# Attention logits of two heads in two row halves of the array, running sums and mask as a bias tile

## The chip, the core and the metric

One core of a Trainium2 chip runs the whole kernel. Five engines work side by side, each in the order of its own instruction queue: TensorE (PE in the profile; its weight loads are listed apart as PEld), VectorE (DVE), ScalarE (ACT), GpSimd (POOL) and SyncE (SP, which here only issues transfers). They wait for each other by semaphores. The metric is the device time of one execution in microseconds (us); less is better. "Before" is the median of 3 runs.

## What is computed

A decoder trunk of two layers over 256 tokens of width 1024, all in float32: a recurrent (RG-LRU) layer first, then a layer of forgetting attention. Each layer has a SwiGLU FFN of half weight in front of its mixer and another behind it. The part at issue is the attention of the second layer: 16 heads of 64, queries in two blocks of 128, and a running sum `c` of log forget gates per head that is added for the query and subtracted for the key.

```python
def shared_kv(h, g, w_kv, w_f, b_f):
    hn = rms_norm(h, g)
    kv = (hn @ w_kv).reshape(Bn, S, 2, N_HEADS, HEAD_DIM)
    k, v = ...
    log_f = jax.nn.log_sigmoid((hn @ w_f + b_f).astype(jnp.float32))
    c = jnp.cumsum(log_f, axis=1).transpose(0, 2, 1)

def forgetting_attention(xq, w_q, w_o, k, v, c):
    q = (xq @ w_q).reshape(...).transpose(0, 2, 1, 3) * (HEAD_DIM ** -0.5)
    for blk in range(S // Q_BLOCK):
        logits = jnp.einsum('bhqd,bhkd->bhqk', q[:, :, q0:end], k[:, :, :end])
        logits = logits + c[:, :, q0:end, None] - c[:, :, None, :end]
        logits = jnp.where(kpos[None, :] <= qpos[:, None], logits, -jnp.inf)
        p = jax.nn.softmax(logits, axis=-1)
        outs.append(jnp.einsum('bhqk,bhkd->bhqd', p, v[:, :, :end]))
    return o @ w_o
```

## The kernel before

**Tokens and products.** The 256 tokens are two tiles of 128, `t` = 0 and 1. Weights come in units of up to 128x1024 floats by transfers that SyncE issues (`load_raw`, 5 `raw` buffers). Each unit is split into a high part `whi` on ScalarE (L173) and a low part `wlo` on VectorE (L177), with 9 buffers each (`WB`). Each product is three fp32r matmuls, high by high, high by low and low by high (`mm3`, L183 to L185). TensorE's order is written out by hand: `run` and `ATT_ORDER` decide which unit of which tile comes next. The other engines' orders come from a scheduler, except where `keep_in_program_order` or `high_priority` is said; the GpSimd work of the attention is kept in program order.

**PSUM.** Eight banks: four `mm` for the products, two `gt` (logits, the gates of the recurrent layer, the transposes of the stream, the running sums), two `tr` (other transposes).

**Keys, queries and the running sums.** The keys are projected right after the recurrent layer, among the units of the next FFN, the queries after that FFN. `heads_T` scales a 128x512 piece of a projection (`htok`, L954, VectorE), transposes it in four pieces (L959, TensorE) and writes even heads by ScalarE (L962) and odd heads by VectorE (L963), so that each head has its 64 features on partitions 0 to 63 of `kT` or `qT`. Two more rows carry the sums: row 64 of `kT` is 1 and row 65 the sum at the key; row 64 of `qT` is the sum at the query and row 65 is -1. So a product over 66 rows gives the logits with both terms. The sums come from `running`: the negated log gates `lf` times a triangle of -1 (`triu`, and `mone` for the first tile's total), copied to `c` (L993) and moved to the row of `kT` by a small transfer on GpSimd's queue (L994). `att_rows` moves `c` and `mone` to the rows of `qT` (L947, L948). The mask is one tile `cmask` of 0 and -1e30.

**The attention of one tile.** Groups of `per` heads: 4 of 128 keys for `t` = 0, 2 of 256 keys for `t` = 1, so each group's logits fill one bank. Four steps per group, each at the place that `ATT_ORDER` gives it (`l0` is the logits of a group of tile 0; a bare digit is a unit of weights for that tile):

- `l`, `logits`: the products into one `gt` bank (L1063), the mask added on the diagonal block (L1064) and the negative maximum (L1066) on VectorE, then per head an exponential with its sum on ScalarE (L1071)
- `n`, `norm`: reciprocal of the sums (L1077) and the product with it (L1078) on VectorE
- `t`, `turn`: four transposes (L1084) and a copy to `pT` (L1086)
- `v`, `values`: the products with `v`, two heads side by side in column halves of the array (L1098), and after eight heads the split of the output (L1104, L1105)

**The recurrent layer's gates** (`gw_unit`, L761) are block-diagonal fp32 products over tiles of 126 rows. The parts that cross a tile's edge are products over rows 0 to 63 and over rows 64 to 125, issued alternately into two banks. They are not touched by the change.

**GpSimd** also computes the two small steps of each RMS norm, `nv` (L198) and `rstd` (L200), whose results VectorE and ScalarE need as scales.

## Time and profile before

| | us |
|---|---|
| median of 3 runs | 987.98 (987.91 to 988.26) |
| profiled execution, its own time | 987.51 |
| its span, first to last instruction | 985.8 |
| logits products L1063, busy, by tile | 4.3 and 8.2 |
| mask and maximum on VectorE (L1064, L1066), busy, by tile | 5.5 and 8.9 |

The granted TensorE clock was 0.998 of full speed over the span.

How to read it: busy time is the time in which an engine executes an instruction. Matmuls are pipelined, so their busy times overlap; the chain of waits, which follows the work back from the last instruction, gives each piece of the path once. In a row of grouped instructions, `gt<-kT,qT` names the tile written and the tiles read, `66*128 66x256` the weights' rows and columns and the moving operand, `x32` the count. Behind the bar stand the busy time in us, the mean of one in ns, and the idle time before them with what ended it. An fp32 matmul of the program is two matmuls in the trace.

### The profile page before, as it was taken

To read this page: it belongs to the slowest core of one execution; us is meant where nothing else is said; L and a number is where in the kernel's file an instruction comes from. 1 tells how busy PE (TensorE), PEld (TensorE's weight loads), DVE (VectorE), ACT (ScalarE), POOL (GpSimd) and SP (SyncE) were. 2 spreads that over 40 slices of the span, in tenths; PEclk is the share of its full clock that TensorE was granted. 3 is DMA by queue.
4 is the path that set the end of the run, shared out by engine and by line. 5 is a ranking of instruction groups with operands and counts; after the bars stand their busy time and mean duration, and the time that the engine had idled before them with its cause. 6 is when DMAs were issued, how large, how long until landed. Compare 5 with 4: busy or idle time off the path is not lost.

```text
span 985.8 us, 13028 instructions
## 1 busy us (share of the span) xinstructions
PE 978.0 (99%) x4777; PEld 813.4 (83%) x4777; DVE 616.6 (63%) x791; ACT 530.1 (54%) x753; POOL 47.2 (5%) x92
## 2 busy tenths in 40 slices
PE   9999999999999999999999999999999999999997
PEld 6888888898978888888898888888888788888886
DVE  6666554678997555554686655554488876555542
ACT  7545443568986544443564444544366755444431
POOL 2400000100003000000100000000020000000000
PEclk9999999999999999999999999999999999999999
DMA  8787766565346877666567676665552467776631
GB/s 292 263 266 249 222 210 192 158 192 162 117 126 198 241 211 212 217 207 188 131 203 242 186 220 213 214 213 185 190 173 64 123 210 235 213 213 212 205 117 43
DMA packets 99558, 190.45 MB, mean 193 GB/s; under 512 B 12734, under 2 KB 32614, under 8 KB 99494
## 3 DMA queue, kind: packets, MB, share of 16 engines
q1 hardware_dynamic: 98054, 188.95, 61.3%
q8 instruction: 38, 0.62, 0.3%
q10 hardware_dynamic: 608, 0.53, 0.2%
q0 software_dynamic: 832, 0.12, 0.1%
q14 instruction: 26, 0.21, 0.1%
HBM read 176.95 MB, written 1.05 MB: 181 GB/s over the span
## 4 chain that ended last, share of the span: by engine, by line
PE 98%; issue 1%; DVE 1%; ACT 0%; POOL 0%; POOLq 0%; DVEq 0%; ACTq 0%
PE mm L183 29%; PE mm L185 29%; PE mm L184 28%; PE gt L761 2%; PE tr L525 1%; PE mm L1195 1%; PE gt L1063 1%; PE mm L190 1%; PE mm L191 1%; PE mm L192 1%; PE mm L1098 1%; PE tr L1084 1%; PE gt L214 1%; PE tr L127 0%; PE tr L959 0%
## 5 line engine op out<-in xcount | busy, mean ns | idle before, releaser
L177 DVE TENSOR_TENSOR wlo<-raw,whi 128x1024 fp32r<-128x1024 f32 (+5 forms) x329 | 395.3, 1207 | 268.3 <-ACT whi L173 266.1
L173 ACT ACTIVATE whi<-raw 128x1024 fp32r<-128x1024 f32 (+5 forms) x329 | 341.9, 1046 | 314.8 <-PE mm L185 260.2
L183 PE MATMUL mm<-whi,xhi 128*128 128x512 f32 (+1 forms) x768 | 301.2, 392 | 0.0
L185 PE MATMUL mm<-whi,xlo 128*128 128x512 f32 (+1 forms) x768 | 298.2, 388 | 0.3 <-DVE xlo L228 0.3
L184 PE MATMUL mm<-wlo,xhi 128*128 128x512 f32 (+1 forms) x768 | 297.9, 388 | 0.0
L185 PEld LDWEIGHTS mm<-whi,xlo 128*128 128x128 f32 x768 | 144.2, 188 | 30.7 <-DVE xlo L228 0.7
L183 PEld LDWEIGHTS mm<-whi,xhi 128*128 128x128 f32 x768 | 144.2, 188 | 29.4 <-issue 1.3
L184 PEld LDWEIGHTS mm<-wlo,xhi 128*128 128x128 f32 x768 | 144.3, 188 | 28.2 <-DVE wlo L177 0.3
L183 PE MATMUL mm<-whi,hhi 128*128 128x512 f32 x352 | 137.9, 392 | 0.0
L185 PE MATMUL mm<-whi,hlo 128*128 128x512 f32 x352 | 137.1, 389 | 0.0
L184 PE MATMUL mm<-wlo,hhi 128*128 128x512 f32 x352 | 137.0, 389 | 0.0
L185 PEld LDWEIGHTS mm<-whi,hlo 128*128 128x128 f32 x352 | 66.1, 188 | 13.9
L184 PEld LDWEIGHTS mm<-wlo,hhi 128*128 128x128 f32 x352 | 66.1, 188 | 13.3
L183 PEld LDWEIGHTS mm<-whi,hhi 128*128 128x128 f32 x352 | 66.1, 188 | 13.3
L510 DVE SCALAR_TENSOR_TENSOR prod<-mm,rstd,sil 128x512 f32<-128x512 f32 (+1 forms) x48 | 33.8, 705 | 35.2 <-PE mm L185 31.1
L498 ACT ACTIVATE sil<-mm,rstd 128x512 f32<-128x512 f32 (+1 forms) x48 | 31.2, 651 | 38.7 <-PE mm L185 34.2
L198 POOL TENSOR_SCALAR nv<-ss 128x1 f32<-128x1 f32 x22 | 9.6, 435 | 716.3 <-ACT junk L205 716.3
L529 ACT ACTIVATE hhi<-tr 128x512 fp32r<-128x512 f32 (+1 forms) x48 | 24.8, 558 | 13.8 <-PE tr L525 13.8
L205 ACT ACTIVATE junk<-mm 128x512 bf16<-128x512 f32 x24 | 14.3, 595 | 32.7 <-PE mm L185 32.6
L272 DVE TENSOR_TENSOR t<-mm,gb 128x512 f32<-128x512 f32 x24 | 16.1, 685 | 24.7 <-ACT junk L205 24.6
L530 DVE TENSOR_TENSOR hlo<-tr,hhi 128x512 fp32r<-128x512 f32 (+1 forms) x48 | 29.2, 640 | 2.6 <-ACT hhi L529 2.6
L183 PE MATMUL mm<-whi,zhi 128*128 128x340 f32 (+2 forms) x80 | 28.2, 353 | 0.0
(196 smaller groups left out, 885.8 us busy)
## 6 DMA issues: line engine op xcount, KB each, us to landing
raw<-in_ffn_w_down_dram SPq DMA_DIRECT2D x88, 512.0 KB
raw<-in_ffn_w_up_dram SPq DMA_DIRECT2D x80, 512.0 KB
raw<-in_ffn_w_gate_dram SPq DMA_DIRECT2D x78, 512.0 KB
prr<-prod SPq DMA_DIRECT2D x40, 256.0 KB
raw<-in_rg_w_in_dram SPq DMA_DIRECT2D x10, 504.0 KB
raw<-in_rg_w_out_dram SPq DMA_DIRECT2D x10, 504.0 KB
raw<-in_ffn_w_gate_dram SPq DMA_DIRECT2D x19, 256.0 KB
raw<-in_ffn_w_up_dram SPq DMA_DIRECT2D x16, 256.0 KB
```

What stands on the lines that cost most here:

```text
L173: up = nc.scalar.activation(hi[:parts, c:c + m], rawv[:, c:c + m], AF.Copy)
L177: nc.vector.tensor_tensor(lo[:parts, c:c + m], rawv[:, c:c + m], hi[:parts, c:c + m].bitcast(F32), ALU.subtract)
L183: nc.tensor.matmul(ps, xh, wh, start=first, stop=False)
L184: nc.tensor.matmul(ps, xh, wl, start=False, stop=False)
L185: nc.tensor.matmul(ps, xl, wh, start=False, stop=last)
L205: nc.scalar.activation(junk[:, :src.shape[1]], src, AF.Square, scale=f, accum_out=acc)
L272: nc.vector.tensor_tensor(t1[n], pf[n], gb[:, n * 512:(n + 1) * 512], ALU.mult)
L498: nc.scalar.activation(s[:, :nn], ps, AF.Silu, scale=rs[t][:, 0:1])
L510: nc.vector.scalar_tensor_tensor(pr[:, :nn], ps, rs[t][:, 0:1], s, ALU.mult, ALU.mult)
L529: nc.scalar.activation(hv, tp[:, :nn], AF.Copy)
L530: nc.vector.tensor_tensor(lv, tp[:, :nn], hv.bitcast(F32), ALU.subtract)
L761: nc.tensor.matmul(ps[j][:w, g * S:(g + 1) * S], wv[rows, o:o + w], xc[rows, k, :], start=start, stop=stop, skip_group_check=True)
```

## The change

- **Layout.** `kT` and `qT` keep what the transposes give: even heads on partitions 0 to 63, odd heads on 64 to 127, 8 columns of pairs in place of 16 heads. One ScalarE copy of 128x512 writes both, and VectorE's copy of odd heads is gone. The two rows for the sums are gone.
- **Logits.** Heads are taken alternately from the lower and the upper 64 rows, into two `gt` banks, one per half. A group takes both banks.
- **Bias.** `bias0` (128x16x128) and `bias1` (128x16x256) hold, for each query, head and key, the sum at the query less the sum at the key, and -1e30 where the key is later than the query. `lf` is the negated log gate, so the sums that go to the DRAM tile `crows` are negated. They come back broadcast to all partitions on GpSimd's queue, GpSimd subtracts `cq`, the negated sum at the query (one value per partition and head), and masks the last 128 columns with `affine_select`, four heads at a time. `bias0` is made in `running(0)`, `bias1` in `att_rows`.
- **Running sums.** `triu` is now +1, `mone` is a column `one`. `running` makes the sums twice: by rows of heads (`pc`, as before) and by partitions of tokens (`pq`, copied to `cq`).
- **One operation per head.** `tensor_tensor_reduce` on VectorE writes the negated sum of logits and bias to `pe` in SBUF and its minimum, which is the negated maximum, to `mx`. It is emitted as two instructions, the operation and a read of its accumulator. The exponential reads `pe` with scale -1 and bias `mx`.
- **Buffers.** The query's `htok` uses the `pT` buffers.

```diff
 def kv_tiles():
-        kv["kT"] = lp.tile([HA, NH, S], F32, name="kT")
+        kv["kT"] = lp.tile([P, NH // 2, S], F32, name="kT")
...
+        kv["bias0"] = lp.tile([P, NH, P], F32, name="bias0")
+        kv["rows"] = dram.tile([NH, S], F32, name="crows")
...
+    def bias_of(v, t, h0, hn):
+        keep = tc.keep_in_program_order
+        w = v.shape[2]
+        keep(nc.gpsimd.tensor_tensor(v, v, kv["cq"][t][:, h0:h0 + hn].unsqueeze(2).to_broadcast([P, hn, w]), ALU.subtract))
+        d = v[:, :, w - P:]
+        keep(nc.gpsimd.affine_select(out=d, in_=d, compare_op=ALU.is_ge, fill=NEG, base=0,
+                                     pattern=[[0, hn], [-1, P]], channel_multiplier=1))

     def att_rows():
         tc.keep_in_program_order(nc.scalar.activation(warm, mhalf, AF.Exp))
-        for t in range(2):
-            tc.keep_in_program_order(nc.gpsimd.dma_start(att["q"][t][HD:HD + 1, :, :], kv["c"][t]))
-            tc.keep_in_program_order(nc.gpsimd.dma_start(att["q"][t][HD + 1:HA, :, :], kv["mone"][:NH, :]))
+        v = att["bias1"]
+        tc.keep_in_program_order(nc.gpsimd.dma_start(v, kv["rows"].partition_broadcast(P)))
+        for h0 in range(0, NH, 4):
+            bias_of(v[:, h0:h0 + 4, :], 1, h0, 4)
...
             with tc.high_priority():
-                nc.scalar.activation(to[:, :, 0, :], tp[:HD, :].rearrange("p (a b) -> p a b", a=4), AF.Copy)
-                nc.vector.tensor_copy(to[:, :, 1, :], tp[HD:, :].rearrange("p (a b) -> p a b", a=4))
+                nc.scalar.activation(dst[:, 4 * n:4 * n + 4, :], tp.rearrange("p (a b) -> p a b", a=4), AF.Copy)
...
     def running(t):
-        pc = gtbank()
+        pc, pq = gtbank(), gtbank()
+        one = kv["one"].to_broadcast([P, P])
         if t == 1:
-            nc.tensor.matmul(pc[:NH, :P], kv["lf"][0], kv["mone"], start=True, stop=False)
+            nc.tensor.matmul(pc[:NH, :P], kv["lf"][0], one, start=True, stop=False)
         nc.tensor.matmul(pc[:NH, :P], kv["lf"][t], kv["triu"], start=t == 0, stop=True)
-        nc.vector.tensor_copy(kv["c"][t], pc[:NH, :P])
-        nc.gpsimd.dma_start(kv["kT"][HD + 1:HA, :, t * P:(t + 1) * P], kv["c"][t])
+        if t == 1:
+            nc.tensor.matmul(pq[:, :NH], one, kv["lf"][0], start=True, stop=False)
+        nc.tensor.matmul(pq[:, :NH], kv["triu"], kv["lf"][t], start=t == 0, stop=True)
+        ct = pools["f"].tile([NH, P], F32, name=f"c{t}")
+        nc.vector.tensor_copy(ct, pc[:NH, :P])
+        nc.vector.tensor_copy(kv["cq"][t], pq[:, :NH])
+        nc.gpsimd.dma_start(kv["rows"][:, t * P:(t + 1) * P], ct)
+        if t == 0:
+            nc.gpsimd.dma_start(kv["bias0"], kv["rows"][:, :P].partition_broadcast(P))
+            for h0 in range(0, NH, 4):
+                bias_of(kv["bias0"][:, h0:h0 + 4, :], 0, h0, 4)
...
     def logits(hg):
             hds = range(hg * per, (hg + 1) * per)
-            ps = gtbank().rearrange("p (a b) -> p a b", a=per)
+            ps = [gtbank() for _ in range(2)]
             for j, hd in enumerate(hds):
-                nc.tensor.matmul(ps[:, j, :], att["q"][t][:, hd, :], kv["kT"][:, hd, :nk * P], start=True, stop=True)
-            nc.vector.tensor_tensor(ps[:, :, t * P:], ps[:, :, t * P:], mask, ALU.add)
+                r = slice(j % 2 * HD, (j % 2 + 1) * HD)
+                nc.tensor.matmul(ps[j % 2][:, j // 2 * w:(j // 2 + 1) * w], att["q"][t][r, hd // 2, :],
+                                 kv["kT"][r, hd // 2, :w], start=True, stop=True, skip_group_check=True)
             mx = spool.tile([P, 4], F32, tag="mx", name=nm("mx"))
-            nc.vector.tensor_reduce(mx[:, :per], ps, AX.X, ALU.max, negate=True)
...
             for j, hd in enumerate(hds):
-                nc.scalar.activation(pe[:, j, :], ps[:, j, :], AF.Exp, bias=mx[:, j:j + 1],
+                nc.vector.tensor_tensor_reduce(pe[:, j, :], ps[j % 2][:, j // 2 * w:(j // 2 + 1) * w], bias[:, hd, :], -1.0,
+                                               -NEG, ALU.add, ALU.min, mx[:, j:j + 1])
+            for j, hd in enumerate(hds):
+                nc.scalar.activation(pe[:, j, :], pe[:, j, :], AF.Exp, bias=mx[:, j:j + 1], scale=-1.0,
```

More of the change, by code (lines that the diff above doesn't have):

```diff
@@ L26 @@
 HD = 64
-HA = HD + 2
 EPS = 1e-6
@@ L54, in trunk_kernel @@
     psum = ctx.enter_context(tc.tile_pool(name="psum", bufs=1, space=bass.MemoryType.PSUM))
+    dram = ctx.enter_context(tc.tile_pool(name="dram", bufs=1, space=bass.MemoryType.DRAM))
     uid = [0]
@@ L919, in kv_tiles @@
         lp = ctx.enter_context(tc.tile_pool(name="kv", bufs=1, reuse_waits="tile"))
-        kv["kT"] = lp.tile([HA, NH, S], F32, name="kT")
+        kv["kT"] = lp.tile([P, NH // 2, S], F32, name="kT")
         kv["v"] = [lp.tile([P, D], F32, name=f"v{t}") for t in range(2)]
         kv["lf"] = [lp.tile([P, NH + 8], F32, name=f"lf{t}")[:, :NH] for t in range(2)]
-        kv["c"] = [lp.tile([NH, P], F32, name=f"c{t}") for t in range(2)]
+        kv["cq"] = [lp.tile([P, NH], F32, name=f"cq{t}") for t in range(2)]
@@ L925, in kv_tiles @@
         kv["bfb"] = lp.tile([P, NH], F32, name="bfb")
-        for n in ("triu", "mone", "cmask"):
-            kv[n] = lp.tile([P, P], F32, name=n)
+        kv["triu"] = lp.tile([P, P], F32, name="triu")
+        kv["one"] = lp.tile([P, 32], F32, name="one")[:, :1]
+        kv["bias0"] = lp.tile([P, NH, P], F32, name="bias0")
+        kv["rows"] = dram.tile([NH, S], F32, name="crows")
     def kv_constants():
         keep = tc.keep_in_program_order
-        triu, cm = kv["triu"], kv["cmask"]
+        triu = kv["triu"]
@@ L933, in kv_constants @@
         keep(nc.gpsimd.dma_start(kv["bfb"], A["b_fgate"].partition_broadcast(P)))
-        keep(nc.gpsimd.memset(triu, -1.0))
+        keep(nc.gpsimd.memset(triu, 1.0))
         keep(nc.gpsimd.affine_select(out=triu, in_=triu, compare_op=ALU.is_ge, fill=0.0, base=0,
                                      pattern=[[1, P]], channel_multiplier=-1))
-        keep(nc.gpsimd.memset(kv["mone"], -1.0))
-        keep(nc.gpsimd.memset(cm, 0.0))
-        keep(nc.gpsimd.affine_select(out=cm, in_=cm, compare_op=ALU.is_ge, fill=NEG, base=0,
-                                     pattern=[[-1, P]], channel_multiplier=1))
@@ L941, in kv_constants @@
-        keep(nc.gpsimd.memset(kv["kT"][HD:HA, :, :], 1.0))
+        keep(nc.gpsimd.memset(kv["one"], 1.0))
+    def bias_of(v, t, h0, hn):
[5 more added lines that the diff above has]
+                                     pattern=[[0, hn], [-1, P]], channel_multiplier=1))
@@ L943, in att_rows @@
     def att_rows():
         tc.keep_in_program_order(nc.scalar.activation(warm, mhalf, AF.Exp))
-        for t in range(2):
-            tc.keep_in_program_order(nc.gpsimd.dma_start(att["q"][t][HD:HD + 1, :, :], kv["c"][t]))
-            tc.keep_in_program_order(nc.gpsimd.dma_start(att["q"][t][HD + 1:HA, :, :], kv["mone"][:NH, :]))
-    def heads_T(pool, ps, t, n, scale, dst):
-        tok = pool.tile([P, 512], F32, tag="prod", name=nm("htok"), bufs=2)
+        v = att["bias1"]
+        tc.keep_in_program_order(nc.gpsimd.dma_start(v, kv["rows"].partition_broadcast(P)))
@@ L953, in heads_T @@
+        for h0 in range(0, NH, 4):
+            bias_of(v[:, h0:h0 + 4, :], 1, h0, 4)
+    def heads_T(pool, ps, t, n, scale, dst, tag, bufs):
+        tok = pool.tile([P, 512], F32, tag=tag, name=nm("htok"), bufs=bufs)
         with tc.high_priority():
@@ L959, in turn @@
                 nc.tensor.transpose(tp[:, j * P:(j + 1) * P], tok[:, j * P:(j + 1) * P], ident)
-            to = dst[:HD, 8 * n:8 * n + 8, :].rearrange("p (a two) b -> p a two b", two=2)
             with tc.high_priority():
-                nc.scalar.activation(to[:, :, 0, :], tp[:HD, :].rearrange("p (a b) -> p a b", a=4), AF.Copy)
-                nc.vector.tensor_copy(to[:, :, 1, :], tp[HD:, :].rearrange("p (a b) -> p a b", a=4))
+                nc.scalar.activation(dst[:, 4 * n:4 * n + 4, :], tp.rearrange("p (a b) -> p a b", a=4), AF.Copy)
         defer(2, turn)
     def post_k(n):
-        return lambda t, ps: heads_T(pools["f"], ps, t, n, 1.0, kv["kT"][:, :, t * P:(t + 1) * P])
+        return lambda t, ps: heads_T(pools["f"], ps, t, n, 1.0, kv["kT"][:, :, t * P:(t + 1) * P], "prod", 2)
     def post_f(t, ps):
@@ L1045, in att_tiles @@
         ap = pools["a"]
-        att["q"] = [ap.tile([HA, NH, P], F32, name=f"qT{t}") for t in range(2)]
+        att["q"] = [ap.tile([P, NH // 2, P], F32, name=f"qT{t}") for t in range(2)]
+        att["bias1"] = ap.tile([P, NH, S], F32, name="bias1")
         att["oh"] = [ap.tile([P, 8, P], F32R, name=f"oh{t}") for t in range(2)]
@@ L1054, in attention @@
         per = 4 // nk
-        mask = kv["cmask"].unsqueeze(1).to_broadcast([P, per, P])
+        bias = kv["bias0"] if t == 0 else att["bias1"]
+        w = nk * P
         box = {}
@@ L1060, in logits @@
             hds = range(hg * per, (hg + 1) * per)
-            ps = gtbank().rearrange("p (a b) -> p a b", a=per)
+            ps = [gtbank() for _ in range(2)]
             for j, hd in enumerate(hds):
-                nc.tensor.matmul(ps[:, j, :], att["q"][t][:, hd, :], kv["kT"][:, hd, :nk * P], start=True, stop=True)
-            nc.vector.tensor_tensor(ps[:, :, t * P:], ps[:, :, t * P:], mask, ALU.add)
+                r = slice(j % 2 * HD, (j % 2 + 1) * HD)
+                nc.tensor.matmul(ps[j % 2][:, j // 2 * w:(j // 2 + 1) * w], att["q"][t][r, hd // 2, :],
+                                 kv["kT"][r, hd // 2, :w], start=True, stop=True, skip_group_check=True)
             mx = spool.tile([P, 4], F32, tag="mx", name=nm("mx"))
-            nc.vector.tensor_reduce(mx[:, :per], ps, AX.X, ALU.max, negate=True)
             if hds[0] % 8 == 0:
                 box["sm"] = spool.tile([P, 8], F32, tag="sm", name=nm("sm"))
-            pe = ap.tile([P, per, nk * P], F32, tag="pe", name=nm("pe"), bufs=3)
+            pe = ap.tile([P, per, w], F32, tag="pe", name=nm("pe"), bufs=3)
             for j, hd in enumerate(hds):
-                nc.scalar.activation(pe[:, j, :], ps[:, j, :], AF.Exp, bias=mx[:, j:j + 1],
+                nc.vector.tensor_tensor_reduce(pe[:, j, :], ps[j % 2][:, j // 2 * w:(j // 2 + 1) * w], bias[:, hd, :], -1.0,
+                                               -NEG, ALU.add, ALU.min, mx[:, j:j + 1])
+            for j, hd in enumerate(hds):
+                nc.scalar.activation(pe[:, j, :], pe[:, j, :], AF.Exp, bias=mx[:, j:j + 1], scale=-1.0,
                                      accum_out=box["sm"][:, hd % 8:hd % 8 + 1])
@@ L1109, in post_q @@
     def post_q(n):
-        return lambda t, ps: heads_T(pools["a"], ps, t, n, HD ** -0.5, att["q"][t])
+        return lambda t, ps: heads_T(pools["a"], ps, t, n, HD ** -0.5, att["q"][t], "pT", 4)
     for n in range(2):
```

## The prediction

> **What bounds the kernel now.** I read the page first: busy times, then the chain that ended last.

> ```profile
> span 985.8 us, 13028 instructions
> PE 978.0 (99%) x4777; PEld 813.4 (83%) x4777; DVE 616.6 (63%) x791; ACT 530.1 (54%) x753; POOL 47.2 (5%) x92
> PE 98%; issue 1%; DVE 1%; ACT 0%; POOL 0%; POOLq 0%; DVEq 0%; ACTq 0%
> ```

> TensorE is busy for 99% of the span and carries 98% of the chain. Then I cut out the stages by windows: the end of the second layer's first FFN (714 to 732), the attention of the first token tile (732 to 753), and of the second (753 to 784). The columns are the stretch, its length, the busy time of PE, PEld, DVE, ACT and POOL, the clock, the DMA share and GB/s.

> ```profile
> 714.00:732.00 18.00, 18.00 (x89) 15.07 (x88) 17.32 (x22) 14.44 (x23) 6.57 (x12) 1.00 0.60 204
> 732.00:753.00 21.00, 20.99 (x131) 17.77 (x130) 16.02 (x25) 12.19 (x41) 0.00 (x0) 1.00 0.33 103
> 753.00:784.00 31.00, 31.00 (x209) 24.65 (x209) 24.94 (x46) 21.74 (x56) 0.86 (x2) 1.00 0.29 85
> ```

> The attention has no gap on TensorE, so the change can win only by making TensorE's own work there shorter. No stall is there to be removed. VectorE has 5.0 us free in the first window (21.00 - 16.02) and 6.1 us in the second (31.00 - 24.94): that is the cover for whatever it is late with.

> **The logits on TensorE.** The chain of waits gives each piece's start, its length and its line.

> ```profile
> 738.49 0.89 PE gt L1063 x8
> ...
> 741.20 0.44 PE tr L1084 x4
> ...
> 753.17 0.86 PE gt L1063 x4
> 754.03 0.59 PE mm L1098 x8
> 754.62 0.59 PE tr L1084 x4
> ...
> 758.05 0.43 PE mm L183
> 758.47 0.23 PE mm L184
> ...
> 766.31 1.02 PE mm L1098 x16
> ```

> An fp32 product is two passes. Four heads of 128 columns take 8 passes, 0.89 us (0.11 each); two heads of 256 columns take 4, 0.86 us (0.215 each). There are 4 groups of the first kind and 8 of the second: 3.56 + 6.88 = 10.44 us. The kernel already runs 64-row products in two halves of the array, in the gates (L761):

> ```profile
> 258.16 2.79 PE gt L761 x16
> ...
> 268.04 0.34 PE mm L183
> 268.38 0.15 PE mm L184
> ```

> ```profile
> L761 PE MATMUL gt<-xc,gw 64*126 64x256 f32 x20 | 5.6, 402 | 0.0
> L1063 PE MATMUL gt<-kT,qT 66*128 66x256 f32 x32 | 8.2, 378 | 0.0
> ```

> Of the 16 passes of 2.79 us, 8 use all rows: 8 x 0.215 = 1.72. The other 8 use 64 or 62 rows and take the remaining 1.07. One after the other they would take 1.72, two at a time 0.86. So they do run in pairs, and 0.21 us goes with entering that mode. Leaving it costs as well: the next fp32r product takes 0.34 where its neighbour takes 0.15, so 0.19. The halves by columns (L1098) say the same: 16 passes less 8 is 0.43 for 4 pairs, so a block of 8 has 0.16 of entry; behind it a transpose block takes 0.59 in place of 0.44 (0.15), an L183 0.43 in place of 0.23 (0.20).

> The new group is then 4 pairs of 0.11, or 2 of 0.215, 0.43 either way, plus 0.21: 0.64. Twelve of them are 7.68, 2.76 less than now. The exits come on top. By the order of the changed program, three groups of the first tile are followed by a weight product (0.20 each) and four of the second by a transpose block (0.15 each), 1.20 together; the other five are followed by L1098, whose own entry is paid today. That leaves a gain of 1.56 us. Bounds of the switches: 0, a gain of 10.44 - 12 x 0.43 = 5.3, and 0.3 an entry, which leaves 0.5. I take the L761 value, the same operation in the same mode.

> [...]

> **The running sums.** `running` keeps its products into `pc` and gets three more into `pq`, 128 weight columns by 16 moving: 6 passes.

> ```profile
> 517.78 0.32 PE gt L992 x2
> 518.10 0.35 PE mm L183
> ```

> The first product behind it pays 0.20 today (0.35 for 0.15). Then `pq` is entered by a full-width block (0.15 as above), with 2 and 4 passes at 0.11, and no 0.20 behind: +0.17 and +0.39, 0.56 us. TensorE in all: -1.56 + 0.56 = -1.0.

> **VectorE.** Per group a mask addition and a maximum go; per head come one combined operation and a read of its accumulator, which this trace does not have.

> ```profile
> L1064 DVE TENSOR_TENSOR gt<-gt,cmask 128x512 f32<-128x512 f32 x4 | 2.8, 694 | 1.5 <-PE gt L1063 1.5
> L1066 DVE TENSOR_REDUCE mx<-gt 128x4 f32<-128x512 f32 x4 | 2.7, 686 | 0.1
> L1064 DVE TENSOR_TENSOR gt<-gt,cmask 128x256 f32<-128x256 f32 x8 | 3.4, 422 | 0.9 <-PE gt L1063 0.8
> L1066 DVE TENSOR_REDUCE mx<-gt 128x2 f32<-128x512 f32 x8 | 5.5, 682 | 0.0
> L963 DVE COPY qT<-tr 64x512 f32<-64x512 f32 x4 | 2.8, 693 | 1.7 <-ACT qT L962 1.6
> L249 DVE SCALAR_TENSOR_TENSOR xlo<-gt,gT,xhi 128x128 fp32r<-128x128 f32 x16 | 4.5, 340 | 0.4 <-ACT xhi L246 0.4
> L1071 ACT ACTIVATION_READ_ACCUMULATOR pe<-gt,mx 128x1 f32 x32 | 6.4, 202 | 0.0
> ```

> Nearest rows: 0.34 for 128 columns (L249), 0.42 for 256 (L1064), 0.20 for the read (ScalarE's). First tile: 4 x 0.54 = 2.16 for 1.38 before; second: 2 x 0.62 = 1.24 for 1.10; over 4 and 8 groups +3.1 and +1.1; the four `qT` copies (L963) take 2.8 away. +1.4 us against 11.1 free: hidden. Lower bound: no read cost, -5.0 us, worth nothing either, since TensorE does not wait. Upper bound: the combined operation at twice its row, 16 x 0.34 + 16 x 0.42 = 12.2 more, rival F. ScalarE's exponentials read SBUF in place of PSUM, with the same number and sizes.

> **Both banks.** A group now holds both `gt` banks until its combined operations are done, and the next group waits. The tightest place:

> ```profile
> 762.33 0.44 PE tr L959 x4
> ...
> 769.31 0.86 PE gt L1063 x4
> ...
> 771.99 0.86 PE gt L1063 x4
> ```

> ```profile
> 769.54 1.22 DVE L177 TENSOR_TENSOR wlo<-raw,whi 128x1024 fp32r<-128x1024 f32 x1
> ```

> The group would end at 769.31 + 0.64 = 769.95, VectorE is in L177 until 770.76, two operations of 0.62 end at 772.0: level with the next group's 771.99. The other spacings are the same or wider, so 0 to 0.5 us in all; I take 0.3. Behind a late group stand the transposes and the weight products of TensorE's fixed order.

> **The bias tiles on GpSimd.** Gone are the `cmask` and `kT` fills and four 8 KB transfers. New are, per tile, a broadcast from DRAM (1 MB for `bias0`, 2 MB for `bias1`), then four subtractions and four masks.

> ```profile
> 714.39 0.30 POOL L198 TENSOR_SCALAR nv<-ss 128x1 f32<-128x1 f32 x1 [182.85 <-ACT junk L205]
> ```

> `bias0` starts behind L992 of the first tile (517.78), GpSimd has nothing to do for the 182.85 us up to 714.39, and the first logits come after 732: hidden. Its share with VectorE there meets weights that are split several units ahead. `bias1` is on a clock. It takes the place of the small transfers behind the `rstd` of the second tile:

> ```profile
> 726.05 0.58 POOL L947 DMA_DIRECT2D qT<-c  x1
> ```

> ```profile
> GB/s 292 263 266 249 222 210 192 158 192 162 117 126 198 241 211 212 217 207 188 131 203 242 186 220 213 214 213 185 190 173 64 123 210 235 213 213 212 205 117 43
> ```

> ```profile
> 754.17 0.42 DVE L1064 TENSOR_TENSOR gt<-gt,cmask 128x256 f32<-128x256 f32 x1
> ```

> With 292 GB/s as what the queues can move (the highest slice), 88 are free until 732 (0.5 MB) and 189 after (1.6 MB in 8.3 us): it lands near 740. The first piece is needed at 754.17, so a first subtraction and mask of up to 4 us leave 10 us. The `rstd` of the other tile, queued behind the transfer, stands ahead of the subtractions, so nothing of the stage waits behind them on GpSimd until the `nv` after the attention. Price of a piece:

> ```profile
> L737 POOL MEMSET gw<- 126x1008 f32 x5 | 4.6, 960 | 0.0
> L939 POOL TENSOR_SCALAR_AFFINE_SELECT cmask<-cmask 128x128 f32<-128x128 f32 x1 | 0.3, 292 | 0.1
> ```

> A subtraction over 1024 elements: at least 0.96 (writing alone), at most three times that (two reads, a write), 2.9; a mask of 512: 0.29 to 1.17. Four pieces: 5.0 to 16.3 us; I take the middle, 10.6. [...]

> This work runs at about 740 to 752 beside VectorE, and the two share something:

> ```profile
> 728.74 1.02 POOL L198 TENSOR_SCALAR nv<-ss 128x1 f32<-128x1 f32 x1 [0.68 <-ACT junk L205]
> ```

> ```profile
> 727.32 2.35 DVE L177 TENSOR_TENSOR wlo<-raw,whi 128x1024 fp32r<-128x1024 f32 x2
> ```

> The same `nv` takes 0.30 at 714.39 and 1.02 beside L177, and ends just after L177 does (729.76 and 729.67): GpSimd waits for VectorE. Whether VectorE waits for GpSimd no row shows. Bounds: 0, and rival B's 3.5 us (gains are excluded, as nothing of VectorE's is shortened by it). I take 0.2, near the end that the row supports.

> **Sum.** -1.0 + 0.3 + 0.2 = -0.5 us. The profiled execution took 987.51 us (span and launch), the median of the runs is 987.98; on the latter's scale the forecast is 987.5.

> **Rivals.** B, slower: VectorE's operations on two SBUF tiles (L177, and the normalisation L1078) wait for GpSimd's running subtraction or mask. The place is 740 to 753, the price 10.6 us of GpSimd work that no longer overlaps, against 5.0 us free and three `qT` copies of 0.69 (only the fourth's transposes, at 762.33, come later): 3.5 us late at the transposes. Without the 0.2 the forecast is 987.3, so 990.8; at the ends of the GpSimd price 987.3 to 996.5 (5.7 us more). It decides from 7.1 us of blocked time on. [...] C, faster: the mode switches are hidden, gain 5.3 - 0.56 = 4.7, 983.3; against it stand L761 and L1098 alike. D: `bias1` lands after 750, because the weight loads keep their rate or the broadcast reads slowly; each us beyond is one lost, say 5: 992.5. E, the change does not do what it says, the halves run one after the other: the entries and exits are pure cost, 12 x 0.21 + 1.20 + 0.56 = +4.3, 992.3; the 1.07 of L761 speaks against it. F: the combined operation at twice its row: 12.2 + 1.4 - 11.1 = 2.5 late, 990.0.

> **Chances.** The forecast 0.56, B 0.24, C 0.08, F 0.05, D 0.04, E 0.03. About 0.2% (2 us) is what a measurement of this kernel can tell from no change. Faster: C and a 0.03 tail of the forecast, 0.11. Slower: two thirds of B, D, E, half of F, a 0.04 tail of the forecast, 0.30. Same: 0.59. Range for 8 in 10: from 985.0, between the forecast and C, to 992.3, above B's own value and at E's.

> **What would show it.** Right: twelve logits blocks of 0.6 to 0.7 us in the chain, with 0.15 to 0.20 more on what follows them; PE without idle time in 732 to 784; the `bias1` transfer landing by 745. Wrong: VectorE's L177 or L1078 well over 1.22 and 0.69 us while GpSimd subtracts (B); blocks of 0.43 (C) or 0.9 (E); TensorE idle on a `gt` bank or before a transpose; a combined operation above 0.5 us for 256 columns (F).

## The result, and the profile after

The changed kernel takes 990.94 us (median of 10 runs, 987.62 to 991.54), the kernel before 987.94 beside it: a ratio of 1.0026, 95% interval 1.0017 to 1.0036. It is slower by 0.3%. The page of its profiled execution (989.56 us) begins:

```profile
span 987.8 us, 13077 instructions
PE 977.4 (99%) x4783; PEld 808.7 (82%) x4783; DVE 614.5 (62%) x825; ACT 531.2 (54%) x753; POOL 66.1 (7%) x103
PE 96%; issue 1%; DVE 1%; ACT 0%; POOL 0%; POOLq 0%; DVEq 0%; ACTq 0%
```

TensorE has less to do (977.4 us, 978.0 before), the span is 2.0 us longer, and TensorE's share of the chain fell from 98% to 96%. By stretches (columns as in the prediction's windows):

```profile
714.00:735.00 21.00, 21.00 (x104) 17.59 (x103) 18.49 (x24) 15.48 (x24) 5.21 (x9) 1.00 0.62 229
735.00:756.00 21.00, 18.37 (x118) 14.02 (x117) 17.30 (x46) 12.73 (x41) 13.51 (x8) 1.00 0.46 153
756.00:790.00 34.00, 34.00 (x231) 24.17 (x230) 24.77 (x63) 24.68 (x59) 1.65 (x4) 1.00 0.29 81
```

In these stretches TensorE is idle for 2.63 us, all of it in the attention of the first tile, where GpSimd now works for 13.51 us. The TensorE rows there, in order of time (start, length, what; in brackets the idle time before it and what ended it):

```profile
745.06 0.71 PE L1082 MATMUL gt<-kT,qT 64*128 64x128 f32 x8
...
747.94 0.40 PE L185 MATMUL mm<-whi,xlo 128*128 128x512 f32 x1
750.97 0.71 PE L1082 MATMUL gt<-kT,qT 64*128 64x128 f32 x6 [2.63 <-DVE mx L1089]
```

The fourth group of logits waits for its two `gt` banks, which the third group's combined operations have not read yet. Why VectorE is late is in its own rows and in GpSimd's (two views of the same execution):

```profile
738.80 1.92 DVE L1099 TENSOR_TENSOR pe<-pe,sm 128x512 f32<-128x512 f32 x1
...
741.49 2.69 DVE L177 TENSOR_TENSOR wlo<-raw,whi 128x1024 fp32r<-128x1024 f32 x1
...
745.14 4.48 DVE L177 TENSOR_TENSOR wlo<-raw,whi 128x1024 fp32r<-128x1024 f32 x2
```

```profile
738.28 1.90 POOL L945 TENSOR_TENSOR bias<-bias,cq 128x1024 f32<-128x1024 f32 x1 [7.02 <-DMA bias<-crows]
740.25 0.98 POOL L947 TENSOR_SCALAR_AFFINE_SELECT bias<-bias 128x512 f32<-128x512 f32 x1
741.20 1.90 POOL L945 TENSOR_TENSOR bias<-bias,cq 128x1024 f32<-128x1024 f32 x1
743.17 1.50 POOL L947 TENSOR_SCALAR_AFFINE_SELECT bias<-bias 128x512 f32<-128x512 f32 x1
744.64 2.32 POOL L945 TENSOR_TENSOR bias<-bias,cq 128x1024 f32<-128x1024 f32 x1
```

A normalisation takes 1.92 us (0.69 elsewhere) and ends 0.5 us after GpSimd's subtraction. A split (L177) takes 2.69 (1.22 elsewhere): it starts inside a subtraction and ends 1.1 us after that one's end at 743.10. The mask behind the subtraction takes 1.50 in place of 0.64 and ends 0.5 us after the split (744.67 and 744.18). As these rows read, each engine waits for the operation that the other has in flight, and the two take turns.

How much the stage lost is read between two rows of the same kind on either side of it: the last `nv` ahead of the attention and the first behind it. Before, that is 782.46 - 728.74 = 53.72 us (the first of these rows is quoted in the prediction):

```profile
782.46 0.30 POOL L198 TENSOR_SCALAR nv<-ss 128x1 f32<-128x1 f32 x1 [52.05 <-ACT junk L205]
```

After, 784.57 - 729.61 = 54.96:

```profile
729.61 1.01 POOL L198 TENSOR_SCALAR nv<-ss 128x1 f32<-128x1 f32 x1 [2.15 <-ACT junk L205]
...
784.57 0.30 POOL L198 TENSOR_SCALAR nv<-ss 128x1 f32<-128x1 f32 x1 [32.49 <-ACT junk L205]
```

So +1.24 us in the stage. This distance is called the stage below.

### The profile page after: what moved, and what is told of

Its sections match the earlier page's. It is cut to its first block, busy times and chain, and to the rows that moved or that the text cites. A ratio compares the mean times of both kernels' runs of the same rounds, so it can differ in the third digit from the quotient of the medians.

```text
span 987.8 us, 13077 instructions
## 1 busy us (share of the span) xinstructions
PE 977.4 (99%) x4783; PEld 808.7 (82%) x4783; DVE 614.5 (62%) x825; ACT 531.2 (54%) x753; POOL 66.1 (7%) x103
## 4 chain that ended last, share of the span: by engine, by line
PE 96%; issue 1%; DVE 1%; ACT 0%; POOL 0%; POOLq 0%; DVEq 0%; ACTq 0%
PE mm L183 29%; PE mm L185 28%; PE mm L184 28%; PE gt L761 2%; PE tr L525 1%; PE mm L1216 1%; PE mm L190 1%; PE mm L191 1%; PE mm L192 1%; DVE wlo L177 1%; PE gt L1082 1%; PE gt L214 1%; PE mm L1119 1%; PE tr L1105 1%; PE tr L127 0%
## 5 line engine op out<-in xcount | busy, mean ns | idle before, releaser
L177 DVE TENSOR_TENSOR wlo<-raw,whi 128x1024 fp32r<-128x1024 f32 (+5 forms) x329 | 400.2, 1222 | 270.1 <-ACT whi L173 267.9
L183 PE MATMUL mm<-whi,xhi 128*128 128x512 f32 (+1 forms) x768 | 301.3, 392 | 0.0
L184 PE MATMUL mm<-wlo,xhi 128*128 128x512 f32 (+1 forms) x768 | 297.9, 388 | 0.0
L183 PEld LDWEIGHTS mm<-whi,xhi 128*128 128x128 f32 x768 | 144.1, 188 | 29.8 <-issue 1.3
L184 PEld LDWEIGHTS mm<-wlo,xhi 128*128 128x128 f32 x768 | 144.2, 188 | 28.3 <-DVE wlo L177 0.3
L183 PE MATMUL mm<-whi,hhi 128*128 128x512 f32 x352 | 137.8, 392 | 0.0
L184 PE MATMUL mm<-wlo,hhi 128*128 128x512 f32 x352 | 137.0, 389 | 0.0
L183 PEld LDWEIGHTS mm<-whi,hhi 128*128 128x128 f32 x352 | 66.1, 188 | 13.4
L184 PEld LDWEIGHTS mm<-wlo,hhi 128*128 128x128 f32 x352 | 66.1, 188 | 13.4
L198 POOL TENSOR_SCALAR nv<-ss 128x1 f32<-128x1 f32 x22 | 9.6, 435 | 689.0 <-ACT junk L205 689.0
L205 ACT ACTIVATE junk<-mm 128x512 bf16<-128x512 f32 x24 | 14.3, 596 | 32.5 <-PE mm L185 32.2
L183 PE MATMUL mm<-whi,zhi 128*128 128x340 f32 (+2 forms) x80 | 28.2, 353 | 0.0
```

The source lines that it names most:

```text
L177: nc.vector.tensor_tensor(lo[:parts, c:c + m], rawv[:, c:c + m], hi[:parts, c:c + m].bitcast(F32), ALU.subtract)
L183: nc.tensor.matmul(ps, xh, wh, start=first, stop=False)
L184: nc.tensor.matmul(ps, xh, wl, start=False, stop=False)
L205: nc.scalar.activation(junk[:, :src.shape[1]], src, AF.Square, scale=f, accum_out=acc)
```

## The experiments

All ratios are against the kernel before, run beside each. The edits add and remove lines, so the line numbers shift by a few from kernel to kernel.

**1. No GpSimd work on `bias1`**:

```diff
-        for h0 in range(0, NH, 4):
-            bias_of(v[:, h0:h0 + 4, :], 1, h0, 4)
```

> The changed kernel without any GpSimd work on bias1 (no subtraction of the query's sum, no mask: the second tile attends to later keys too); the transfer stays. Theory 1, VectorE's operations on two SBUF tiles and GpSimd exclude each other: L177 and the normalisation are back at 1.22 and 0.69 us in the attention of the first tile, the 2.6 us in which TensorE is idle there are gone, the stage ends about 2.6 us earlier against the rest than with the work, time 987.0 to 987.8. Theory 2, the stall is made by the combined operation or by the two gt banks: the idle time stays above 1.5 us, time 989.5 to 991.

986.60 us, ratio 0.9990 (0.9981 to 0.9999), a little below the range expected. The two rows of VectorE's groups in 735 to 756, and the window:

```profile
L177 DVE TENSOR_TENSOR wlo<-raw,whi 128x1024 fp32r<-128x1024 f32 x3 | 3.7, 1224 | 0.8 <-ACT whi L173 0.8
L1097 DVE TENSOR_TENSOR pe<-pe,sm 128x512 f32<-128x512 f32 x5 | 3.5, 691 | 0.1
```

```profile
735.00:756.00 21.00, 21.00 (x139) 15.73 (x139) 13.55 (x52) 14.06 (x46) 0.00 (x0) 1.00 0.43 149
```

The stall is gone and both operations have their old length. The stage takes 781.39 - 729.38 = 52.01, 1.71 less than before: with GpSimd out of it the change gains what its logits save. Banks and combined operation, which are unchanged here, make no stall by themselves: TensorE is busy for 21.00 of the 21.00 us. What GpSimd's work costs is 54.96 - 52.01 = 2.95 us: 2.63 of idle time, and most of the rest in the group behind it, which takes 0.92 us in the chain in place of 0.65.

**2. The subtraction of `bias1` left out, its masks kept** (L945 for `t` = 0 only).

> The changed kernel with bias1 masked and its subtraction left out (the sum at the query is one value per row of the softmax and cancels there). Theory 1: of some 10.9 us of GpSimd work beside VectorE about 3.5 stay, below the 7.1 us from which it decides, so TensorE is idle for at most 0.5 us, time 987.2 to 988.2. Theory 2: as the changed kernel, 989.5 to 991.

986.49 us, ratio 0.9989 (0.9980 to 0.9998), a little below the range expected. TensorE has no idle time, and the stage is 782.01 - 729.96 = 52.05. The three splits of 735 to 760 take 1.30 on average, in place of 1.22 without the masks; VectorE has that to spare.

```profile
738.60 2.91 POOL L948 TENSOR_SCALAR_AFFINE_SELECT bias<-bias 128x512 f32<-128x512 f32 x4 [6.99 <-DMA bias<-crows]
```

**3. The masks of `bias1` twice, subtractions kept.**

```diff
-        keep(nc.gpsimd.affine_select(out=d, ...))
+        for _ in range(1 + t):
+            keep(nc.gpsimd.affine_select(out=d, ...))
```

> The changed kernel with each mask of bias1 applied twice, four more operations of 0.6 to 1.0 us on GpSimd. Theory 1: 2.5 to 4 us more that cannot overlap with VectorE, all of it beyond the cover, so TensorE is idle for 5 us or more in 735 to 760 and the time is 993 to 995.5. Theory 2: as the changed kernel, 990 to 991.5, since nothing waits for GpSimd but the first tile of bias1.

987.84 us, ratio 1.0004 (0.9995 to 1.0013): a miss. More GpSimd work than in the changed kernel, and a smaller loss. VectorE's rows:

```profile
738.58 2.31 DVE L1100 TENSOR_TENSOR pe<-pe,sm 128x512 f32<-128x512 f32 x1
...
741.65 1.52 DVE L177 TENSOR_TENSOR wlo<-raw,whi 128x1024 fp32r<-128x1024 f32 x1
...
743.29 2.18 DVE L1100 TENSOR_TENSOR pe<-pe,sm 128x512 f32<-128x512 f32 x1
...
745.40 3.22 DVE L177 TENSOR_TENSOR wlo<-raw,whi 128x1024 fp32r<-128x1024 f32 x2
```

Here the splits met short masks (0.6 to 1.0 us) where they met subtractions (1.9) in the changed kernel. So it is not the sum of GpSimd's work that counts: as these rows read, each VectorE operation on two SBUF tiles waits for what GpSimd has in flight, then GpSimd waits for it. The subtraction that starts at 742.06, during the split of 741.65 to 743.17, takes 2.86 in place of 1.90 and ends at 744.92; the normalisation that starts during it, at 743.29, takes 2.18 in place of 0.69 and ends at 745.47.

**4. The subtractions alone, and 5. the subtractions twice** (in 5 the masks stay and each subtraction comes a second time).

> The changed kernel with the subtractions on bias1 and without its masks (the second tile attends to later keys too). Theory 1: four subtractions, 1.9 us each by themselves, 7.6 us beside a cover of 7.1 us. TensorE is idle for 0 to 1.5 us in the attention of the first tile, 986.6 to 988.4. If it is not the sum of GpSimd's work that decides but the alternation with the masks (each change of engine waits once), the idle time is 0 and the time that of no_work1, 986.6.

> The changed kernel with each subtraction on bias1 made twice (the sum at the query cancels in the softmax however often it is taken away). Theory 1: 7.6 us more of GpSimd work that reads SBUF, all beyond the cover, and the pieces for the second tile come later: TensorE idle for 6 to 11 us in 735 to 770, a stretch of half clock behind it in the profile, 995 to 1000. Against it: half clock without more idle time, or idle time below 4 us.

991.52 us, ratio 1.0041 (1.0029 to 1.0054), and 992.14, 1.0048 (1.0035 to 1.0060). Both are misses in size: the first was to cost up to 1.5 us of idle time and cost 3.15, the second 6 to 11 and cost 3.52. TensorE's row behind the stall, in runs 3, 4 and 5:

```profile
749.97 0.92 PE L1083 MATMUL gt<-kT,qT 64*128 64x128 f32 x8 [1.85 <-DVE mx L1090]
```

```profile
751.53 1.44 PE L1084 MATMUL gt<-kT,qT 64*128 64x128 f32 x8 [3.15 <-DVE mx L1091]
```

```profile
752.00 0.92 PE L1083 MATMUL gt<-kT,qT 64*128 64x128 f32 x8 [3.52 <-DVE mx L1090]
```

Five profiles together give a rule for this place. "Lost" is by how much the two normalisations and three splits ahead of the third group's operations exceed 5.05 us (2 x 0.69 + 3 x 1.224):

| kernel | lost by VectorE | TensorE idle | difference |
|---|---|---|---|
| masks twice | 4.18 | 1.85 | 2.3 |
| changed | 4.96 | 2.63 | 2.3 |
| changed, second profile (run 7) | 5.31 | 2.97 | 2.3 |
| subtractions alone | 5.59 | 3.15 | 2.4 |
| subtractions twice | 5.85 | 3.52 | 2.3 |

The cover, which is what VectorE can lose before TensorE waits, is 2.3 to 2.4 us, and behind it each us lost is one of idle TensorE. Run 6 below, which has no stall, shows most of it directly: there VectorE waits 0.44 and 0.75 us among these operations, and 1.41 from the last combined operation on the third group to the first on the fourth, against 0.59 behind the stall of the changed kernel, so 0.8 more; an estimate of 2.0 from these rows. In the changed kernel (two of the splits are one row) an operation loses no more than what GpSimd still has to do on the operation in flight: 1.23 us with 1.38 left (the normalisation at 738.80), 1.47 with 1.61 (the split at 741.49), 0.23 with 0.37 (the normalisation at 744.30, 0.92 long). Five operations would then wait only five times; as measured, doubling the subtractions adds 0.9 us (5.85 - 4.96) and not 7.6. The rule was read from these five profiles; no later run was made to test it.

**6. Fills in place of the work**: eight GpSimd fills of 1024 that only write `bias1`, at the same place.

> The changed kernel with GpSimd's subtractions and masks on bias1 replaced by fills of the same pieces, each twice (8 fills of 1024, about 7.8 us of GpSimd work that only writes; the second tile attends without sums and mask). If GpSimd and VectorE exclude each other whatever GpSimd does, L177 and the normalisation are lengthened and TensorE is idle for 0.5 to 1.5 us, 987.3 to 988.2. If it is GpSimd's reading that collides with VectorE's second SBUF operand, L177 stays at 1.22 us, TensorE is not idle, and the time is that of no_work1, 986.6 (within 0.4).

986.58 us, ratio 0.9989 (0.9980 to 0.9997), stage 782.21 - 730.14 = 52.07, no idle time. GpSimd's group and VectorE's in 735 to 760:

```profile
L957 POOL MEMSET bias<- 128x1024 f32 x8 | 7.5, 955 | 7.3 <-DMA bias<-crows 7.1
```

```profile
L177 DVE TENSOR_TENSOR wlo<-raw,whi 128x1024 fp32r<-128x1024 f32 x3 | 3.7, 1224 | 0.8 <-ACT whi L173 0.8
L1100 DVE TENSOR_TENSOR pe<-pe,sm 128x512 f32<-128x512 f32 x5 | 3.5, 690 | 0.1
```

7.5 us of GpSimd beside VectorE, and nothing lengthened: 1.22 us a split and 0.69 a normalisation, against up to 2.69 and 1.92 beside the subtractions of the changed kernel. Of the GpSimd work of these runs it is that which reads `bias1` that collides, not that which only writes it. In the changed kernel too only operations with both inputs in SBUF were lengthened: L1089 (one input in PSUM) kept 0.28 us beside a subtraction (at 741.28, beside that of 741.20).

**7. The changed kernel once more.**

> The changed kernel once more. Its timed runs lay at 987.6 to 991.5, the profiled one at 989.56 with 2.6 us of idle TensorE; the second time GpSimd's masks were applied twice the idle time was 1.9, so the amount depends on which engine comes first each time. Theory 1 expects the idle time of TensorE in the attention of the first tile to be another amount in this profile (0.5 to 5 us), and the profiled time to follow it one to one: time of the profile = 986.6 + idle time, within 0.4. If the times move and the idle time does not, a slower clock makes the spread.

990.71 us (987.45 to 992.41, 12 runs), ratio 1.0025 (1.0016 to 1.0034). The profiled execution took 991.20 with 3.0 us of idle time, where the sum gave 989.6: a miss. The rest is TensorE's clock (the figure behind POOL) just after the stall. First the profile above, then this one:

```profile
749.00:753.00 4.00, 2.03 (x13) 1.74 (x14) 3.22 (x16) 2.48 (x12) 3.01 (x2) 1.00 0.80 224
753.00:756.40 3.40, 3.40 (x26) 2.40 (x24) 2.15 (x8) 2.43 (x9) 0.00 (x0) 1.00 0.12 45
```

```profile
753.00:756.40 3.40, 3.40 (x18) 2.40 (x17) 1.57 (x7) 2.04 (x8) 0.00 (x0) 0.52 0.11 42
756.40:760.00 3.60, 3.60 (x27) 2.52 (x25) 1.47 (x5) 1.42 (x5) 0.00 (x0) 1.00 0.00 0
```

```profile
753.24 0.43 PE mm L184
753.66 0.43 PE mm L185
754.09 0.85 PE tr L967 x4
754.95 1.05 PE mm L1119 x8
```

For 3.4 us the clock is halved (0.52, and 1.00 from 756.40 on), 18 matmuls run where 26 did, a product takes 0.43 for 0.23 and a transpose block 0.85 for 0.44. That is about 1.6 us (3.4 x 0.48), and it explains the stage: 786.24 - 729.37 = 56.87, 1.9 more than in the first profile, of which 0.3 are idle time. What starts such a stretch and what ends it was not shown. Runs 4 and 5 have the same behind their stalls, run 5 a clock of 0.58 in 753 to 757, run 4 the longest, an estimate of 6.8 us at half clock by these rows (4 x (0.23 + 0.50 + 0.12) = 3.4 lost):

```profile
749.00:753.00 4.00, 1.47 (x9) 1.25 (x9) 2.90 (x12) 1.65 (x8) 0.00 (x0) 0.77 0.64 194
753.00:757.00 4.00, 4.00 (x14) 2.98 (x16) 2.25 (x12) 2.05 (x9) 0.00 (x0) 0.50 0.18 68
757.00:761.00 4.00, 4.00 (x30) 2.62 (x27) 1.08 (x4) 1.50 (x3) 0.00 (x0) 0.88 0.00 0
```

Of the 22 timed runs of this kernel, 14 have a mean granted clock of 0.998 or less and took 990.6 to 992.4; the other 8 have 0.999 or 1.000 and took 987.5 to 989.7. Ten of the 14 have 0.997 or less, and none of the runs of the kernel before beside these experiments is under 0.998. That most runs have the half clock and so the median holds it is inferred from this; only two were profiled, and what the three runs below 988 look like inside is open.

**8. Without the sums by token**: no `pq`, no `cq`, no subtraction in either tile.

> The changed kernel without the sums by token: no pq products, no cq, no subtraction for bias0 and bias1, masks as they are. Theory 1: as masks_only1, and the 0.56 us of pq on TensorE are saved as well, so the offset against the kernel before, 0.7 us higher behind 517 to 545 in the changed kernel, stays within 0.1; time 986.5 to 987.6, level with the kernel before or up to 0.15% faster. If the 0.7 us come from elsewhere (the combined work of GpSimd on bias0 at 535 to 546), the offset rises by the part that is not pq even so.

991.45 us, ratio 1.0043 (1.0030 to 1.0055): a miss. No stall is to be found: the stage is 784.27 - 732.16 = 52.11. The time is lost at other places, in products that the edit doesn't touch (a part of the FFN ahead of `running` among them), where the trace has 231 ns from start to start in place of 227, and TensorE does 267 matmuls in 430 to 490 where masks_only1 does 272. What had moved with `cq` is the place of every later tile in SBUF.

**9. The same, padded** by the 128 bytes that `cq` took, and **10. masks_only1 moved** by 128 bytes:

```diff
-        kv["one"] = lp.tile([P, 32], F32, name="one")[:, :1]
+        kv["one"] = lp.tile([P, 64], F32, name="one")[:, :1]
```

> The changed kernel without cq as before, but with the column of ones padded by the 128 bytes that cq took, so that every later tile of SBUF lies where it lies in the changed kernel. Without the padding the fp32r products were spaced 231 ns in place of 227 in 425 to 555, 660 to 800 and from 915 on. If the place of the tiles does that, the spacing is back at 227 and the time is 985.8 to 986.5, 0.1 to 0.2% faster than before; the offset behind the running sums is 0.0 to 0.1 in place of 0.67. If it is the chip or the missing work, it stays at 991.

> masks_only1 with the column of ones padded by 128 bytes more, nothing else: every later tile of SBUF lies 128 bytes further. If the place of the tiles made no_cq slow, the fp32r products are again spaced about 231 ns in place of 227 in stretches such as 425 to 555 and 660 to 800, and the time is 989 to 992. If it was something else in that kernel, the time is that of masks_only1, 986.5.

986.10 us, ratio 0.9986 (0.9978 to 0.9995), and 992.13, 1.0045 (1.0028 to 1.0062). The place decides: the same padding takes 5.4 us from one kernel and puts 5.6 on the other. The stretch 430 to 490, in masks_only1 and then in the moved one:

```profile
430.00:490.00 60.00, 60.00 (x272) 49.68 (x271) 32.26 (x35) 27.58 (x35) 2.13 (x4) 1.00 0.56 168
```

```profile
430.00:490.00 60.00, 60.00 (x266) 48.74 (x266) 31.09 (x33) 26.85 (x34) 2.05 (x4) 1.00 0.54 163
```

TensorE has no gap and its clock is full, yet it does 266 matmuls where it did 272. Which tile's place matters was not tried. The kernel before and the changed one do 272 in this stretch, too. From the `nv` at 496 to the one at 715 (497.86 and 718.91 in the moved kernel) it is 221.05 us in the moved kernel, and 218.95 to 219.03 in the changed one and in runs 1 to 7 and 12: the place has no part in what the change lost.

**11. Masks of the second tile made early** (without `cq`, padded): behind `running(1)` GpSimd fetches the last 128 keys, two heads at a time, masks them and keeps them in DRAM; the stage of the query only loads.

```diff
+        else:
+            cut = kv["rows"][:, P:]
+            for h0 in range(0, NH, 2):
+                b = pools["f"].tile([P, 2, P], F32, tag="bb", name=nm("bb"), bufs=1)
+                tc.keep_in_program_order(nc.gpsimd.dma_start(b, cut[h0:h0 + 2, :].partition_broadcast(P)))
+                bias_of(b, 1, h0, 2)
+                tc.keep_in_program_order(nc.gpsimd.dma_start(kv["far"][:, h0:h0 + 2, :], b))
```

> Without cq, and the masked half of bias1 made in pieces right behind the running sums of the second tile, kept in DRAM and loaded with the other half in the stage of the query: GpSimd has no work during the attention. Theory 1: no idle TensorE there, no operation of VectorE lengthened; 985.8 to 986.6, level with no_cq_pad, as the four masks alone fit beside VectorE's 7.1 us of cover. If a mask alone costs VectorE something, staged is up to 0.5 us faster than no_cq_pad.

986.48 us, ratio 0.9988 (0.9980 to 0.9997): level with 9. Four masks, 3.39 us of GpSimd in run 9, fit into the cover: TensorE is busy for 21.00 of the 21.00 us of 735 to 756 with them, and in run 11 without. So 9, the simplest, is a version that beats both kernels, 0.14% below the one before; its stage is 781.30 - 729.24 = 52.06, 1.66 us shorter.

**12. The halves in turn**: in masks_only1 a group's heads of the lower rows first, then those of the upper.

```diff
-            for j, hd in enumerate(hds):
+            for j, hd in sorted(enumerate(hds), key=lambda x: x[0] % 2):
```

> masks_only1 with each group's heads of the lower half of the rows first and those of the upper half behind them, in place of alternating. If two heads run side by side only when their products alternate, a group takes twice 0.43 plus one entry of 0.21, 0.86 to 1.07 us in place of 0.64; twelve groups are 2.6 to 5.2 us longer, 989.1 to 991.7, on a TensorE without gaps. If the halves run side by side whatever the order, or never do, the time stays at 986.5.

986.50 us, ratio 0.9990 (0.9980 to 0.9999), and groups as long as with alternation:

```profile
735.54 0.65 PE gt L1083 x8
...
753.47 0.63 PE gt L1083 x4
```

Eight passes over 66 rows took 0.89 before (L1063 in the prediction). The halves run side by side in either order, here with the four passes of one half issued first.

## Why the prediction was wrong

It forecast no change that can be told (987.5), and the kernel is slower, 990.94. Its own steps:

- **Logits: right.** Twelve groups of 0.64 were forecast, with 0.20 on a weight product and 0.15 on transposes behind them. The chain of the changed kernel:

```profile
735.66 0.65 PE gt L1082 x8
736.31 0.43 PE mm L183
736.73 0.23 PE mm L184
...
756.47 0.63 PE gt L1082 x4
757.10 0.59 PE mm L1119 x8
...
763.12 0.59 PE tr L1105 x4
```

  The gain was to be 1.56 us; the stage without collisions is 1.66 to 1.71 shorter (runs 1, 2, 9). Rivals C (blocks of 0.43) and E (0.9) fall.
- **Running sums: right in kind.** The chain has the old block of the first tile (L999), then that of `pq`:

```profile
517.97 0.32 PE gt L999 x2
518.29 0.33 PE gt L1002 x2
```

   From the `nv` at 496 to the one at 715 it is 218.95 us with `pq`, 218.23 before and 218.33 without it (run 9): 0.6 to 0.7, forecast 0.56. TensorE has no gap there before or after, and 1047 matmuls with `pq` for 1041 before.
- **VectorE: right.** The combined operation takes 0.42 us for 256 columns, as assumed, and 0.28 for 128 (0.34 assumed), and its read less than half of the 0.20 assumed, so rival F falls:

```profile
L1089 DVE CUSTOM_DVE_ANT_0 pe<-gt,bias 128x256 f32<-128x256 f32 x16 | 6.3, 418 | 1.4 <-PE gt L1082 1.2
L1089 DVE CUSTOM_DVE_ANT_0 pe<-gt,bias 128x128 f32<-128x128 f32 x16 | 3.8, 282 | 3.3 <-PE gt L1082 3.3
L1089 DVE DVE_READ_ACCUMULATOR2_ANT mx<- 128x1 f32 x32 | 2.6, 82 | 0.0
```

- **Landing of `bias1`: right.** GpSimd's first subtraction starts on it at 738.28, forecast near 740; rival D falls.
- **Price of GpSimd's work: right.** A subtraction takes 1.90 us and a mask 0.64 where nothing holds them, 10.2 for the four pieces; 10.6 was taken.
- **Both banks: 0 by themselves** (run 1), 0.3 taken. But it is on these banks that TensorE waited, 2.63 us, once VectorE was late.
- **"I take 0.2, near the end that the row supports": this step failed.** The bounds were 0 and 3.5 for VectorE waiting on GpSimd. The row showed GpSimd waiting for VectorE, and no row the reverse; but a row in which one engine waits for the other shows that they share something, and then the reverse is open too. The sum gave it no weight. Measured: 2.95 us.
- **Rival B was what happened**, at 0.24, and its 990.8 is near the median, partly by luck. Its price let all GpSimd work stop VectorE, 10.6 us against a cover of 7.1; in fact five operations lose 5.0 us against a cover of 2.3. Its 3.5 stands for 2.95. And it ends at the `gt` banks of the fourth group rather than at transposes.
- **Not priced at all: the clock.** The stall of 3.0 us in run 7 was followed by 3.4 us at a clock of 0.52, some 1.6 us more, and if the timed runs are read as in run 7, most of them have such a stretch.

The sum for the profiled execution: -1.7 logits, +0.7 `pq`, +2.95 collisions are +1.95, against 987.8 - 985.8 = 2.0 in the span. For the median the inferred half clock comes on top.

## What to carry to other kernels

Work moved to an idle GpSimd was not free beside a VectorE that runs operations on two SBUF inputs: it cost 2.95 us here. Look at what GpSimd's operations read, how long each one is, and which VectorE operations stand ahead of the path just then; here a split took 1.52 us beside masks of 0.6 to 1.0 us and 2.69 beside a subtraction of 1.9, and its usual 1.22 beside fills that only write. Whether the same subtractions in shorter pieces would cost less was not tried. First ask whether the moved work is needed: the sum at the query cancels in the softmax, and without it the change wins (runs 2 and 9; run 8 shows that the place of the tiles can undo it). Beside a stall on a TensorE without gaps, price a stretch at a lower clock behind it: here the stalls of 3.0 to 3.5 us had one of about 3.4 us and more at half clock, those of 1.85 and 2.6 us none.
